# Lane rates, load distances, weight sums and a norm's factor moved in a Hymba encoder layer on one Trainium2 core

## The chip, the cores and the metric

The kernel runs on one core of one Trainium2 chip. The metric is the device time of one execution in microseconds (us), as the median of several runs; less is better. PE is the matmul engine (PEld its weight loads), DVE the vector engine, ACT the scalar engine, POOL the GpSimd engine, and SP the engine whose queue issues most DMA transfers.

## The reference

One layer of a bidirectional encoder for 1024 sample tokens and 256 prompt tokens of width 2048. The two requests share the weights.

```python
hn = rms_norm(x, norm_g)
proj = hn @ w_in                      # 2048 -> 4896 columns
xbc, z_ssd, dt_raw, q, k, v, z_att, mq, z_mem = split_cols(proj, IN_SIZES)
xbc = silu(centred_dwconv(xbc, conv_w, conv_b))          # 5 taps
y = ssd_scan(forward) + ssd_scan(backward) + d_skip * xs  # chunks of 128, 16 heads of 64
yg = (y * silu(z_ssd)).reshape(b, T, 2, 512)
o_ssd = rms_norm(yg, ssd_norm_g)                          # 1024 columns
o_att = window_attention(q, k, v, sink) * silu(z_att)     # 8 heads of 64, 2 kv heads, |t-s| <= 128
mk, mv = split_cols(rms_norm(mem) @ w_mem_kv)
o_mem = softmax(mq @ mk.T) @ mv * silu(z_mem)             # 4 heads of 128, 256 memory rows
return x + concatenate([o_ssd, o_att, o_mem]) @ w_out
```

## The kernel before

**Products.** A product in fp32 is made as three matmuls on operands split into a high and a low part (`wh`, `wl` of the weights, `xH`, `xL` of the activations). A weight tile comes by DMA into `wraw`; `wsplit` makes `wh` on ACT (L206) and `wl` on DVE (L207). The ten token tiles of 128 rows (eight of the sample, two of the prompt) form two groups of five.

**Main blocks.** `block_tok` (matmuls at L258 to L260, 512 columns wide) has the tokens on the partitions and five accumulators `acc`; `block_feat` (L293 to L295, 320 wide) has the features there. `block_pair` (L1236 to L1238) makes a pair of products as seven instead of eight, with sums of weight tiles that `weight_sums` forms on POOL (L1208) from tiles loaded at L1201. In order of time stand: the memory's keys and values; the q block of group 0; the pairs with the input weights; the k, v, dt block and the z and x blocks; the same kind of blocks for group 1; the "o" blocks with the output weights; and the last pairs. A block yields once for each of its 16 steps in depth.

**Lanes.** Beside the main blocks two lanes of generators hold the small work. Lane 0 holds key preparation, window attention (`attn`) and memory attention (`mem_attn`) by tile; lane 1 the row statistics, `dt_prep`, and the scan's two passes (`ssd_up`, `ssd_down`). After each block step `pump` adds the block's two rates from `RATES` (lane 0, lane 1) to what is owed, and takes that many steps of each lane. A `yield` in a lane's generator is the end of such a step. So a number in `RATES` and the number of `yield`s between two operations together say how many block steps, and matmuls, lie between these operations in the program.

**From program to order.** The program order is not the order of the engines: a list scheduler places each instruction by its dependences, the buffers' lives and priorities (`tc.high_priority`), and may bring a transfer forward; `tc.issue_after(marks)` ties some instructions to the last weight split.

**Names used below.** In `attn`: `q` (loaded at L599, squared into `sq` at L602), `qh` (its halves), `pq` (turned in PSUM at L623), `qT` (copied by ACT at L625), `psc` (scores, L641 and L642), `nm` (minus maximum, from DVE at L643), `lg` and `pT` (probabilities, and turned ones, L664). In `mem_attn`: `mq`, `pmq` (turned at L717), `sq` (L722), `mqh` and `mql` (high and low part, L730 on ACT and L732 on DVE), `pms` (scores, L745 to L747), `mpr` (probabilities, L754 and L759), `pmt` (turned, L767). In the scan: `pst` (a chunk's state, L868 to L870), `bh`, `fh`, `fl`, `bth`, `btl` (high and low parts for it, `fh` and `bh` by ACT at L882 among others), `rf` and `rb` (decays, L925 and L931), `py` (a chunk's product, L942), `pyb` (the backward part, L1063), `yd` (the sum), `yss` and `yrs` (sum of squares, and the norm's factor for two groups of 512 columns), `so` (the turned result, L1012).

**The norm of the scan's output.** `ssd_down` squares half of y (`scale=0.5`), takes the root's inverse by `rsqrt` on POOL, multiplies it by 0.5 on POOL (L1081), and leaves the tile in `last_y`. `norm_ssd`, called in the next tile's generator, multiplies the two halves of y by it on DVE (L1001), and `turn_ssd` turns and stores them.

**Refills of the activations' operand.** `run` drives a block. It also takes pieces from `pend`: a piece is loaded by DMA (L188) into one of four buffers `ch`, and some steps later split into `xH` (L197 or L200 on ACT) and `xL` (L198 or L201 on DVE). In each step the oldest loaded piece is split if `lag` of them are in hand, and then one more is loaded. The pieces of the output operand come from `oT` this way: two quads during the second zm block, two during the first "o" block.

Of the kernel before, what the change touches and what calls it, by code (L numbers as in the profile page):

```python
# [16 lines left out]
ALU = mybir.AluOpType  # L17
# [12 lines left out]
RBB = 4  # L30

RATES = ({'kv': (4.0, 1.0), 'z1': (2.2, 1.7)},
         {'kv': (1.5, 1.5), 'x': (2.1, 2.15), 'q': (2.25, 2.5), 'za': (2.15, 2.5), 'z0': (2.1, 2.5),
          'z1': (2.1, 2.55), 'mq': (2.0, 2.7), 'zm': (1.75, 2.75), 'o': (2.15, 2.4)})
FAR = 1e30

UNITS = (0, 8, 1, 9, 2, 10, 3, 11, 4, 12, 5, 13, 6, 7)
# [7 lines left out]
def hymba_encoder_kernel(  # L45
# [7 lines left out]
    V, A, G, T, S = nc.vector, nc.scalar, nc.gpsimd, nc.tensor, nc.sync  # L53
# [361 lines left out]
    def w2(name):  # L415
        return mp.tile([P, 512], F32, tag="wa", name=name, bufs=WA)
# [172 lines left out]
    def attn(t):  # L589
# [8 lines left out]
        q = w2("q")  # L598
        S.dma_start(q, q_d[t])  # L599
        yield  # L600
        sq = w2("sq")
        A.activation(sq, q, AF.Square)  # L602
        ss = sm.tile([P, 8], F32, tag="s8", name="qss", bufs=4)
# [99 lines left out]
    def mem_attn(t):  # L703
# [4 lines left out]
        if grp == 0:  # L708
            S.dma_start(hv(q, 4), mT_d[:, :, tc_])
        else:  # L710
            S.dma_start(q, mq_d[t])
        yield

        def turned():
# [281 lines left out]
    def norm_ssd():  # L996

        if "y" in last_y:
            t, ys, rs = last_y.pop("y")
            for g in range(2):  # L1000
                V.tensor_scalar(out=ys[g], in0=ys[g], scalar1=rs[:, g:g + 1], scalar2=None, op0=ALU.mult)  # L1001
                last_y[g] = t, ys[g]

    def turn_ssd(g):
# [10 lines left out]
    def ssd_down(t):  # L1015
        first = t in (0, NS)
        last = t in (NS - 1, NT - 1)
        tok = slice(t * P, (t + 1) * P)
        ss = sm.tile([P, 2], F32, tag="s2", name="yss", bufs=4)
        if not last:  # L1020
            cc = mp.tile([P, 2, P], F32, tag="btok", name="cc", bufs=1)
            S.dma_start(cc, xbc_d[10:12, :, tok].rearrange("f p c -> p f c"))
        ld = []
        for g in range(2):
            c = slice(g * 512, (g + 1) * 512)

            y = mp.tile([P, 512], F32, tag="ya" if t % 2 else "rf", name="yd", bufs=2)
            S.dma_start(y, yp_d[t][:, c])
            if g == 0 and t < 5:
                z = mp.tile([P, 512], F32R, tag="xs", name="zd", bufs=2)  # L1030
                S.dma_start(hv(z.bitcast(F32), 4), yT_d[:, :, tok])
            else:
                z = mp.tile([P, 512], F32, tag="xs", name="zd", bufs=2)
                S.dma_start(z, z_d[g][t])
            st = None
            if not first:
                st = state[:, c] if last else wb("st2")
                S.dma_start(st, sb_d[t][:, c])
            d = mp.tile([P, 4, P], F32R, tag="rb", name="ydT", bufs=RBB)
            S.dma_start(d.bitcast(F32), yd_d[t][:, 4 * g:4 * g + 4, :])  # L1040
            ld.append((y, z, st, d))

        def diag_in(g):
            ps = psum("pd")
            for j in range(4):
                T.transpose(ps[:, j * P:(j + 1) * P].bitcast(F32R), ld[g][3][:, j, :], identr)
            V.tensor_add(ld[g][0], ld[g][0], ps)

        for _ in range(9 if last else 4):
            yield  # L1050
        norm_ssd()
        diag_in(0)
        yield
        for g in range(2):
            c = slice(g * 512, (g + 1) * 512)
            y, z, st, _ = ld[g]
            if g == 0 and t < 5:
                zr, z = z, psum("pz")
                for j in range(4):
                    T.transpose(z[:, j * P:(j + 1) * P].bitcast(F32R), zr[:, j * P:(j + 1) * P], identr)  # L1060
            if not last:
                pf = psum("pyb")
                T.matmul(pf, cc[:, g, :], state[:, c], start=True, stop=True)  # L1063
                y2 = wb("y3")
                V.tensor_mul(hv(y2), hv(pf), hb(eacs_all[:, t, 16 + 8 * g:24 + 8 * g], 8, 64))
                V.tensor_add(y, y, y2)
            V.tensor_mul(y, y, z)
            if g == 0 and t < 5:
                z = wb("zq")
            A.activation(z, y, AF.Square, scale=0.5, accum_out=ss[:, g:g + 1])  # L1070
            if not first and not last:
                V.tensor_mul(hv(state[:, c]), hv(state[:, c]), hb(cd_all[:, t, 16 + 8 * g:24 + 8 * g], 8, 64))
                V.tensor_add(state[:, c], state[:, c], st)
            yield
            turn_ssd(g)
            if g == 0:
                diag_in(1)
                yield
        rs = sm.tile([P, 2], F32, tag="s2", name="yrs", bufs=4)
        rsqrt(rs, ss, 1.0 / 512, 2)  # L1080
        G.tensor_scalar(out=rs, in0=rs, scalar1=0.5, scalar2=None, op0=ALU.mult)  # L1081
        last_y["y"] = t, [x[0] for x in ld], rs
        yield
        if first:
            for _ in range(3):
                yield
            norm_ssd()
            yield
            yield
            for g in range(2):  # L1090
                turn_ssd(g)
                yield
# [204 lines left out]
    def p_step(j):  # L1297
        if j == 9:
            need(x_rows, [0])
        with ExitStack() as st:  # L1300
            for ins in marks:
                st.enter_context(tc.issue_after(ins))
            if j in (25, 27):
                weight_sums(w_in_pairs, (j - 25) // 2)
            for f, k in sorted(p_plan.get(j, ()), key=lambda x: ((p_split, p_sums, p_fill, p_load).index(x[0]), x[1])):
                f(k)

# [92 lines left out]
    def run(gen, rates, after=None, hold=0, lag=2, extra=None):  # L1400

        for k in gen:
            if after is not None:
                pend.extend(after(k))
            if hold:
                for _ in range(2 if k < KT - 4 else 0):
                    if pend:
                        u = pend.popleft()()
                        next(u)
                        next(u)  # L1410
            else:

                if loaded and (len(loaded) == lag or not pend or k >= KT - 4):
                    next(loaded.popleft())
                if pend and k < KT - 4:
                    loaded.append(pend.popleft()())
                    next(loaded[-1])

            if k >= hold:
                pump(rates)  # L1420
            if extra is not None:
                extra(k)
# [99 lines left out]
    run(block_tok(w_mem_rows(1), 4, ev_mv, places=TURNED), MR[1], extra=p_step)  # L1522

    def tok(name, w, evac, after=None, grp=0):
        run(block_tok(w, 5, evac), RATES[grp][name], after)

    def feat(name, b, evac, grp, after=None, extra=None):
        run(block_feat(f"{name}{b}", evac), [r / 2 for r in RATES[grp][name]], after, lag=3, extra=extra)

    run(block_tok(w_in_rows("q"), 5, ev_raw(q_d, 0), feats=PAIRED, places=PAIRED), (0, 0),  # L1530
        extra=lambda k: p_step(16 + k))
# [197 lines left out]
```

## The time and the profile before

| | |
|---|---|
| median of 3 runs | 1786.98 us (1786.98 to 1789.12) |
| profiled execution | 1787.15 us, span 1785.4 us |
| granted clock of PE | 1.00 in every stretch |
| DMA moved | 301.12 MB, 169 GB/s on the mean |
| HBM | 236.36 MB read, 62.69 MB written |

The span runs from the first to the last instruction that the profiler recorded; 1.75 us of the execution's time lie around it. Lines of the profile are read so. In the list of waits, "PE psc L641 <- ACT qT L625: 0.5, 1, 0.5" says that the matmuls of line 641 that write psc waited for ACT's instruction of line 625 that writes qT: 0.5 us in all, once, 0.5 us at the longest. In the timeline, a row has the start, the duration, the engine, the line, the operation, out<-in by the program's names, the shapes and a count, and in brackets the idle time of the engine before it and what ended that. In a list by tile, the three figures are the least, the median and the greatest duration in ns, and then the first and the last start. Matmuls are pipelined: the distance between two starts says more than a matmul's own duration.

### The profile page before, as it was taken

The numbers are of one execution on the slowest core, as the hardware profiler recorded it, in microseconds if no ns is written. First come the engines' busy times: TensorE is split into PE (matmuls) and PEld (weight loads), VectorE is DVE, ScalarE is ACT, GpSimd is POOL, SyncE is SP. The second block draws the span as 40 slices with busy tenths as digits, with TensorE's granted clock in tenths as the row PEclk, the third lists the DMA queues.
The fourth block names the chain that finished last, engine by engine and source line by source line (L and its number), as shares of the span: only waits on it lengthen the run. The fifth ranks groups of instructions, "written<-read, shape, count | busy, mean of one in ns | idle before, by whom it ended". The sixth has DMA issues, their size and how long they took to land.

```text
span 1785.4 us, 31407 instructions
## 1 busy us (share of the span) xinstructions
PE 1774.2 (99%) x10838; PEld 1605.7 (90%) x10838; DVE 1245.6 (70%) x2358; ACT 921.0 (52%) x2049; POOL 542.2 (30%) x900
## 2 busy tenths in 40 slices
PE   9999999999999999999999999999999999999999
PEld 8888999999998999999889977877988888899999
DVE  5595788888868887778665665556777644766665
ACT  5554455554435766656464565544447533533333
POOL 0105789989710101001001000000100000058775
PEclk9999999999999999999999999999999999999999
DMA  8554454445446644453645645547777764744442
GB/s 305 188 180 124 136 153 148 141 144 162 124 145 211 196 136 138 130 162 112 192 115 172 193 148 165 168 157 250 227 227 239 241 194 140 224 143 148 148 141 78
DMA packets 208208, 301.12 MB, mean 169 GB/s; under 512 B 19569, under 2 KB 86193, under 8 KB 208049
## 3 DMA queue, kind: packets, MB, share of 16 engines
q1 hardware_dynamic: 207904, 299.06, 54.4%
q8 instruction: 85, 1.39, 0.3%
q14 instruction: 75, 0.61, 0.1%
q10 hardware_dynamic: 144, 0.06, 0.0%
HBM read 236.36 MB, written 62.69 MB: 167 GB/s over the span
## 4 chain that ended last, share of the span: by engine, by line
PE 88%; issue 6%; DVE 2%; DMA 2%; ACT 1%; POOL 1%; SPq 0%; ACTq 0%; POOLq 0%; DVEq 0%
PE acc L258 10%; PE acc L259 10%; PE acc L260 10%; PE acc L1238 7%; PE acc L1236 7%; PE acc L1237 7%; PE acc L293 5%; PE acc L295 5%; PE acc L294 5%; PE accm L1237 3%; PE accm L1236 3%; PE accm L1238 3%; PE po L673 1%; PE ppt L663 1%; PE py L942 1%
## 5 line engine op out<-in xcount | busy, mean ns | idle before, releaser
L207 DVE TENSOR_TENSOR wl<-wraw,wh 128x512 fp32r<-128x512 f32 (+1 forms) x480 | 345.4, 721 | 241.0 <-ACT wh L206 234.2
L206 ACT ACTIVATE wh<-wraw 128x512 fp32r<-128x512 f32 (+1 forms) x480 | 292.1, 613 | 307.0 <-PE acc L260 150.4
L258 PE MATMUL acc<-wh,xH 128*128 128x512 f32 (+1 forms) x1088 | 418.7, 385 | 0.2 <-DVE v_all L337 0.2
L259 PE MATMUL acc<-wl,xH 128*128 128x512 f32 (+1 forms) x1088 | 409.7, 377 | 1.1 <-DVE wl L207 1.1
L260 PE MATMUL acc<-wh,xL 128*128 128x512 f32 (+1 forms) x1088 | 410.1, 377 | 0.0
L259 PEld LDWEIGHTS acc<-wl,xH 128*128 128x128 f32 x1088 | 204.6, 188 | 37.7 <-DVE wl L207 2.2
L258 PEld LDWEIGHTS acc<-wh,xH 128*128 128x128 f32 x1088 | 204.5, 188 | 37.7 <-issue 3.3
L260 PEld LDWEIGHTS acc<-wh,xL 128*128 128x128 f32 x1088 | 204.2, 188 | 36.7 <-issue 0.2
L293 PE MATMUL acc<-xH,wh 128*128 128x320 f32 x640 | 202.7, 317 | 0.0
L206 ACT ACTIVATE sh<-ws 128x384 fp32r<-128x384 f32 x176 | 91.4, 523 | 209.0 <-POOL ws L1208 117.1
L294 PE MATMUL acc<-xL,wh 128*128 128x320 f32 x640 | 198.9, 311 | 0.0
L295 PE MATMUL acc<-xH,wl 128*128 128x320 f32 x640 | 198.0, 309 | 0.0
L207 DVE TENSOR_TENSOR sl<-ws,sh 128x384 fp32r<-128x384 f32 x176 | 124.7, 712 | 98.0 <-ACT sh L206 97.7
L1208 POOL TENSOR_TENSOR ws<-wraw 128x128 f32<-128x128 f32 x176 | 110.7, 629 | 212.5 <-DMA wraw<-in_w_in_pairs_dram 92.7
L635 POOL COPY lg<-nsink 128x2 f32<-128x2 f32 x40 | 13.7, 341 | 377.1 <-PE ppt L663 243.6
L293 PEld LDWEIGHTS acc<-xH,wh 128*128 128x128 f32 x640 | 120.2, 188 | 2.6 <-issue 2.2
L294 PEld LDWEIGHTS acc<-xL,wh 128*128 128x128 f32 x640 | 120.3, 188 | 1.7 <-issue 1.4
L295 PEld LDWEIGHTS acc<-xH,wl 128*128 128x128 f32 x640 | 120.2, 188 | 0.6 <-issue 0.5
L1208 POOL TENSOR_TENSOR ws<-wraw,ws 128x128 f32<-128x128 f32 x176 | 116.3, 661 | 13.8
L1208 POOL TENSOR_TENSOR wraw<-wraw 128x128 f32<-128x128 f32 x176 | 110.9, 630 | 13.7
L1208 POOL TENSOR_TENSOR ws<-ws,wraw 128x128 f32<-128x128 f32 x176 | 115.0, 654 | 0.0
L362 DVE SCALAR_TENSOR_TENSOR c<-u,vec,c 128x638 f32<-128x638 f32 (+1 forms) x96 | 90.1, 939 | 9.0 <-ACT c L357 8.6
(437 smaller groups left out, 3942.9 us busy)
## 6 DMA issues: line engine op xcount, KB each, us to landing
wraw<-in_w_in_laid_dram SPq DMA_DIRECT2D x176, 256.0 KB, 2.9
wraw<-in_w_in_pairs_dram SPq DMA_DIRECT2D x112, 256.0 KB, 2.7
wraw<-in_w_out_laid_dram SPq DMA_DIRECT2D x64, 256.0 KB, 3.6
wraw<-in_w_out_pairs_dram SPq DMA_DIRECT2D x64, 256.0 KB, 2.8
rf<-ac SPq DMA_DIRECT2D x40, 256.0 KB, 4.1
rb<-ac SPq DMA_DIRECT2D x40, 256.0 KB, 5.0
wraw<-in_w_mem_laid_dram SPq DMA_DIRECT2D x32, 256.0 KB, 4.2
xst<-in_x_sample_dram SPq DMA_DIRECT2D x20, 256.0 KB, 5.3
```

The source lines that it names most:

```text
L206: a = A.activation(h, raw, AF.Copy)
L207: b = V.tensor_sub(l, raw, h.bitcast(F32))
L258: T.matmul(ps[t][:, :n], sh, h[:, :n], start=(k_ == 0), stop=False)
L259: T.matmul(ps[t][:, :n], sh, l[:, :n], start=False, stop=False)
L260: T.matmul(ps[t][:, :n], sl, h[:, :n], start=False, stop=(k_ == KT - 1))
L293: T.matmul(o, sh, cur["H", q][:, m, c], start=(k == 0), stop=False)
L294: T.matmul(o, sh, cur["L", q][:, m, c], start=False, stop=False)
L295: T.matmul(o, sl, cur["H", q][:, m, c], start=False, stop=(k == KT - 1))
L1208: G.tensor_tensor(out=o, in0=x, in1=y, op=op)
L1236: T.matmul(ps[p], h, xh, start=(k_ == 0), stop=False)
L1237: T.matmul(ps[p], h, xl, start=False, stop=False)
L1238: T.matmul(ps[p], l, xh, start=False, stop=(k_ == 7))
```

## The change

Five edits. The rates of lane 0 in the blocks of `RATES[1]` rise by 2 to 9%; those of lane 1 stay. `attn` and `mem_attn` get one more `yield` between the load of q or mq and its first use. The factor 0.5 of the scan's norm goes from its own POOL instruction into a second scalar of DVE's product. The first two calls of `weight_sums` with the input pairs stand at steps 21 and 23 of the pair plan in place of 25 and 27. The lag of refills is 3 in place of 2 in `block_tok` blocks, and 4 in place of 3 in `block_feat` blocks.

```diff
 RATES = ({'kv': (4.0, 1.0), 'z1': (2.2, 1.7)},
-         {'kv': (1.5, 1.5), 'x': (2.1, 2.15), 'q': (2.25, 2.5), 'za': (2.15, 2.5), 'z0': (2.1, 2.5),
-          'z1': (2.1, 2.55), 'mq': (2.0, 2.7), 'zm': (1.75, 2.75), 'o': (2.15, 2.4)})
+         {'kv': (1.6, 1.5), 'x': (2.2, 2.15), 'q': (2.3, 2.5), 'za': (2.25, 2.5), 'z0': (2.2, 2.5),
+          'z1': (2.2, 2.55), 'mq': (2.1, 2.7), 'zm': (1.9, 2.75), 'o': (2.25, 2.4)})
...
         S.dma_start(q, q_d[t])
         yield
+        yield
         sq = w2("sq")
...
             S.dma_start(q, mq_d[t])
+        yield
         yield
...
-                V.tensor_scalar(out=ys[g], in0=ys[g], scalar1=rs[:, g:g + 1], scalar2=None, op0=ALU.mult)
+                V.tensor_scalar(out=ys[g], in0=ys[g], scalar1=rs[:, g:g + 1], scalar2=0.5, op0=ALU.mult, op1=ALU.mult)
...
         rsqrt(rs, ss, 1.0 / 512, 2)
-        G.tensor_scalar(out=rs, in0=rs, scalar1=0.5, scalar2=None, op0=ALU.mult)
         last_y["y"] = t, [x[0] for x in ld], rs
...
-            if j in (25, 27):
-                weight_sums(w_in_pairs, (j - 25) // 2)
+            if j in (21, 23):
+                weight_sums(w_in_pairs, (j - 21) // 2)
...
-        run(block_tok(w, 5, evac), RATES[grp][name], after)
+        run(block_tok(w, 5, evac), RATES[grp][name], after, lag=3)
...
-        run(block_feat(f"{name}{b}", evac), [r / 2 for r in RATES[grp][name]], after, lag=3, extra=extra)
+        run(block_feat(f"{name}{b}", evac), [r / 2 for r in RATES[grp][name]], after, lag=4, extra=extra)
```

At the weights, the rows of the engines' orders are the same: SP's queue has the first transfer of L1201 (L1202 in the changed kernel) at the same place. On PE, lane groups move by about one block step from the x blocks on. The first place to see is memory tile 7 on PE, where L717 turns its query (pmq) and L745 onward makes its scores (pms); before, the scores come some thirty block matmuls later than the turn:

```order
L258 MATMUL acc<-wh,xH_16293 128x512
L259 MATMUL acc<-wl,xH_16293 128x512
L260 MATMUL acc<-wh,xL_16294 128x512
L745 MATMUL pms<-mkH,mqh 128x256
L746 MATMUL pms<-mkL,mqh 128x256
```

Now, where lines of this function are two further down, the scores come four matmuls behind the turn:

```order
L719 MATMUL pmq<-identr,mq 128x128 x4
L258 MATMUL acc<-wh,xH_15669 128x512
L259 MATMUL acc<-wl,xH_15669 128x512
L260 MATMUL acc<-wh,xL_15670 128x512
L258 MATMUL acc<-wh,xH_15669 128x512
L747 MATMUL pms<-mkH,mqh 128x256
```

So the scores have moved some 28 matmuls nearer to the turn. The second place is attention tile 5 on PE, where L623 turns half a query (pq) and L641 and L642 make the scores (psc); before, fifteen block matmuls stand between, and these are the last:

```order
L258 MATMUL acc<-wh,xH_6938 128x512
L259 MATMUL acc<-wl,xH_6938 128x512
L260 MATMUL acc<-wh,xL_6939 128x512
L641 MATMUL psc<-kT,qT 128x384
L642 MATMUL psc<-kL,qT 128x384
L641 MATMUL psc<-kT,qT 128x384
```

Now three matmuls of the scan (pst) stand between:

```order
L260 MATMUL acc<-wh,xL_6939 128x512
L624 MATMUL pq<-identr,qh 128x128 x4
L870 MATMUL pst<-bh,bth 128x512
L871 MATMUL pst<-bl,bth 128x512
L872 MATMUL pst<-bh,btl 128x512
L642 MATMUL psc<-kT,qT 128x384
```

So the second turn of that query has moved behind the block matmuls, next to the scores.

The third place is ACT's queue where it makes fh, the high part of a scan operand (L882), beside the splits of the operand's pieces (L200), the memory probabilities (L754), a weight split (L206) and the decays (L925); before:

```order
L754 ACTIVATE mpr,mden<-pms,mm,mr 128x256 x2
L831 ACTIVATE cb<-pcb 128x256
L754 ACTIVATE mpr,mden<-pms,mm,mr 128x256 x2
L200 ACTIVATE xH_16109<-chd,vec 128x640 x2
L206 ACTIVATE wh<-wraw 128x512
L200 ACTIVATE xH_16109<-chd,vec 128x640 x2
L925 ACTIVATE rf<-rf,wj_all 128x128 x4
L882 ACTIVATE fh<-xf 128x512
```

Now:

```order
L206 ACTIVATE wh<-wraw 128x512
L200 ACTIVATE xH_16140<-chd,vec 128x640
L833 ACTIVATE cb<-pcb 128x256
L756 ACTIVATE mpr,mden<-pms,mm,mr 128x256 x2
L200 ACTIVATE xH_16140<-chd,vec 128x640
L206 ACTIVATE wh<-wraw 128x512
L884 ACTIVATE fh<-xf 128x512
L200 ACTIVATE xH_16140<-chd,vec 128x640
L927 ACTIVATE rf<-rf,wj_all 128x128 x4
```

So the decays and a split have moved from ahead of fh to behind it.

## The prediction, before the result was known

> **What bounds the kernel now.** I read the page's head first, then the busy time in stretches, then the waits of the matmul engine, and last the timeline at each of them. The head gives the span, and each engine's busy time with its share and its number of instructions:
>
> ```profile
> span 1785.4 us, 31407 instructions
> PE 1774.2 (99%) x10838; PEld 1605.7 (90%) x10838; DVE 1245.6 (70%) x2358; ACT 921.0 (52%) x2049; POOL 542.2 (30%) x900
> ```
>
> PE is busy for 99% of the span. The order of PE's instructions holds the same matmuls in both kernels; the first one that stands elsewhere in the changed kernel is executed at 607 us now, and behind about 1500 us nothing moves any more. So the stretches are cut there, and two narrower ones are added for later use:
>
> ```profile
> core 0: us, PE busy (x) PEld busy (x) DVE busy (x) ACT busy (x) POOL busy (x), PEclk, DMA share, GB/s
> 0.00:607.00 607.00, 604.34 (x3666) 567.10 (x3667) 463.10 (x767) 314.07 (x637) 320.25 (x515) 1.00 0.55 168
> 607.00:1500.00 893.00, 888.03 (x5455) 771.83 (x5454) 596.13 (x1294) 492.64 (x1212) 71.62 (x129) 1.00 0.57 175
> 1500.00:1785.40 285.40, 281.83 (x1721) 266.78 (x1719) 186.38 (x299) 114.25 (x200) 150.32 (x256) 1.00 0.48 149
> 1180.00:1320.00 140.00, 138.62 (x844) 116.61 (x841) 100.39 (x211) 63.87 (x155) 16.26 (x37) 1.00 0.68 212
> ```
>
> In the 893 us that can move at all, PE is idle for 893.00 − 888.03 = 4.97 us, at a granted clock of 1.00. The change takes no matmul away, so what it can win is among these waits, and what it can lose is a new wait of the same kind. In the list of PE's waits (total us, times, longest) these lead in that stretch:
>
> ```profile
> PE pmt L767 <- DVE mpr L759: 1.3, 2, 1.2
> PE pyb L1063 <- ACT so L1012: 0.9, 1, 0.9
> PE pst L868 <- ACT fh L882: 0.8, 1, 0.8
> PE pms L747 <- DVE mql L732: 0.6, 1, 0.6
> PE psc L641 <- ACT qT L625: 0.5, 1, 0.5
> PE pd L1046 <- DVE nm L643: 0.5, 1, 0.5
> ```
>
> They are few and single. A wait also costs somewhat more than its row says, because a busy PE is not PE at its peak:
>
> ```profile
> 726.85 0.40 PE L870 MATMUL pst<-fh,btl 128*128 128x512 f32 x1
> 727.09 0.34 PE L641 MATMUL psc<-kT,qT 128*128 128x384 f32 x1
> 727.26 0.34 PE L642 MATMUL psc<-kL,qT 128*128 128x384 f32 x1
> 728.11 0.45 PE L641 MATMUL psc<-kT,qT 128*128 128x384 f32 x1 [0.51 <-ACT qT L625]
> ```
>
> Two such matmuls start 727.26 − 727.09 = 0.17 us apart when nothing is in the way, and here 728.11 − 727.26 = 0.85 us, so 0.68 us is lost where the row says 0.51, a third more. All PE idle time between 607 and 1500 us is then worth 4.97 to about 6.6 us.
>
> **The change part by part.** *Paired weights fetched sooner.* The transfer is L1201, called from two steps of the pair plan that lie four steps earlier now.
>
> ```profile
> 56.99 0.43 SPq L1201 DMA_DIRECT2D wraw<-in_w_in_pairs_dram  x1
> ```
>
> It goes out at 56.99 us, far ahead of the q block in which the code stands, because the scheduler had already brought it forward. In the new order it stands at the same row of SP's queue, and POOL's sums at the same rows too. Cost and gain: 0. The same holds for all else before 607 us.
>
> *One more lane step between load and use.* The transfers concerned are q and mq, with ACT as the engine that waits:
>
> ```profile
> ACT sq L602 <- DMA q<-q: 5.5, 3, 2.5
> ACT sq L722 <- DMA mq<-mq: 4.0, 2, 2.9
> ```
>
> In SP's new order the ten q loads stand within three rows of their old places, and their first use on ACT moves by 0 to 13 rows, by none or by fewer than five in eight of the ten; the mq loads and uses move as little. The raised rates take back what the extra step gives. ACT has idle time (492.64 of 893 us busy), so its 9.5 us of waits cost PE nothing except where a PE row names ACT, and the one that follows from such a load (pyb behind so, the second row of the list above) keeps its neighbours on ACT, SP and PE. I leave it at 0.
>
> *Pieces of the output operand.* With a longer lag the piece isn't loaded sooner: one is loaded in each step, and filled when three (or four) are in hand rather than two (or three). The splits on ACT and DVE come a step later, with four buffers in the ring as before. Bounds: from −0.8 us to +0.8 us, the size of the one PE wait that the splits take part in:
>
> ```profile
> 1341.91 0.83 ACT L200 ACTIVATE xH<-chd,vec 128x640 fp32r<-128x640 f32 x1 [0.64 <-DMA chd<-oT]
> 1342.64 0.61 ACT L206 ACTIVATE wh<-wraw 128x512 fp32r<-128x512 f32 x1
> 1343.16 1.54 ACT L200 ACTIVATE xH<-chd,vec 128x640 fp32r<-128x640 f32 x2
> 1344.61 1.27 ACT L925 ACTIVATE rf<-rf,wj_all 128x128 f32<-128x128 f32 x4
> 1345.77 0.62 ACT L882 ACTIVATE fh<-xf 128x512 fp32r<-128x512 f32 x1
> 1346.44 0.50 PE L868 MATMUL pst<-fh,bth 128*128 128x512 f32 x1 [0.76 <-ACT fh L882]
> ```
>
> PE waits 0.76 us for fh (the upper half of a state operand), which stands behind splits and four decay products on ACT. In ACT's new order (shown with the change) the decay products and one of the splits stand behind fh, so I take this wait as gone: −0.8 us.
>
> *The norm's half.* The POOL product is removed in all ten tiles; its factor goes into a second scalar of the DVE product L1001.
>
> ```profile
> DVE yd L1001 <- POOL yrs L1081: 18.2, 10, 3.5
> 1190.65 0.70 POOL L124 TENSOR_TENSOR yrs<-yrs,mhalf 128x2 f32<-128x2 f32 x1
> 1191.44 0.23 POOL L1081 TENSOR_SCALAR yrs<-yrs 128x2 f32<-128x2 f32 x1
> 1191.70 0.49 DVE L1001 TENSOR_SCALAR yd<-yd,yrs 128x512 f32<-128x512 f32 x1 [3.46 <-POOL yrs L1081]
> L1001 DVE TENSOR_SCALAR yd<-yd,yrs x20: 470/484/522, 1191.7 to 1500.8; 128x512 f32<-128x512 f32 x20
> L759 DVE TENSOR_SCALAR mpr<-mpr,mden x40: 333/348/356, 826.7 to 1464.9; 128x256 f32<-128x256 f32 x40
> ```
>
> DVE starts 0.26 us behind the POOL product's start; without it, about 0.3 us sooner, 3 us of DVE waiting over ten tiles. The form with two scalars exists already (L759): 348 ns for 256 columns, against 484 ns for 512 in the old form. Two of the former for one of the latter would be 0.21 us more, 4 us of DVE over the 20 products; with one instruction's fixed part in place of two it is near nothing, which I take. What DVE wins reaches PE only where PE waits for DVE: PE is idle for 1.38 us in all of 1180 to 1320 us. Between +1.4 and −1.4 us; I take −0.4, since DVE wins a little and no leading wait names this chain. The Trainium skill's page "Perfetto Trace Analysis", section "Identifying the Most-Contended Engine", speaks against a large gain here: the engine with the highest occupancy is to be improved first, and POOL and DVE are not that. The same section calls the busy time of matmuls a bad measure and takes that of the weight loads instead, which is 771.83 of 893 us here, so that up to 121 us would be open for a better order; the trace speaks against this, since 512-wide matmuls that wait for nothing start 0.24 us apart (726.85 to 727.09) and their loads can't fill that.
>
> *Higher rates.* Groups of lane matmuls are moved by a block step or so, about 3.5 us of PE time. Some of PE's old waits stand where this happens:
>
> ```profile
> 853.14 0.52 PE L767 MATMUL pmt<-identr,mpr 128*128 128x128 f32 x3 [1.16 <-DVE mpr L759]
> 1242.40 0.70 PE L1063 MATMUL pyb<-state,cc 128*128 128x512 f32 x1 [0.90 <-ACT so L1012]
> 1365.08 0.39 PE L747 MATMUL pms<-mkH,mql 128*128 128x256 f32 x1 [0.62 <-DVE mql L732]
> 1401.88 0.41 PE L767 MATMUL pmt<-identr,mpr 128*128 128x128 f32 x2 [0.16 <-DVE mpr L759]
> ```
>
> The two longest (1.16 us at 853, 0.90 at 1242) keep their neighbours on PE and on the engines that they wait for, and stay. At 1365 us one transfer less stands ahead on SP; half goes, −0.3. The pair at 1401 us moves apart, −0.2. Against that stand new short distances. In attention tile 5 the scores (psc) stood 15 block matmuls behind the turned queries that they read (pq), and now three matmuls are left between, as the rows with the change show. This happens in tiles 4 to 7, while tiles 8 and 9 lose such a place. What it costs in the places that have it:
>
> ```profile
> PEld psc L641 <- ACT qT L625: 1.9, 5, 0.8
> ```
>
> A mean of 1.9 / 5 = 0.38 us, from near 0 to 0.8. Four new less two old: +0.8 at the mean; I take +0.4, because the three matmuls cover part. In the same way, in memory tiles 7 and 8 the scores (pms) come four block matmuls behind the turned queries (pmq), where it was some thirty in tile 7. Four block matmuls at 0.24 us give 1.0 us, in which ACT's mqh must land (an estimate of 0.6 us, the 0.62 of fh's split of the same shape). If ACT and DVE are free, nothing is lost; with a queue ahead, up to about 0.9 us each (0.62 by the row at 1365 us, and a third more). I take 0.25 each, +0.5. Last, the memory scores stand nearer to their turns (pmt) in five or so tiles (by the two orders, with PE's times from the trace, some 4 to 6 us where it was 5 to 9); bounds 0 and 1.16 us each by the row at 853 us. The bulk is still wide enough: +0.5.
>
> The sum: −0.8 − 0.4 − 0.3 − 0.2 + 0.4 + 0.5 + 0.5 = −0.3 us. The profiled execution took 1787.15 us (span 1785.4 and 1.75 around it), 0.17 above the median of 1786.98 us. So 1786.9 us against 1787.15, or 1786.7 against the median; I give 1786.9.
>
> **The rivals.** *The waits go (faster).* If the moves take away not three but nearly all of the stretch's PE waits, 4.97 to 6.6 us are won: 1782.2 to 1780.5 us. For it: the waits are single events, each at a place where a queue happened to be long, and 178 pieces on PE have moved. Against: the two longest (853 and 1242 us) keep their order. Chance 0.29.
>
> *The queues of ACT and DVE come due too soon (slower).* A higher rate puts the consumer nearer to the producer on PE, while ACT and DVE serve the same producer behind weight splits. If every shortened place stalls in full: four scores by 0.8, two memory scores by 0.9, five turns by 1.16, together 10.8 us, less the 1.7 won: 1796 us; with half of them 1791.7 us. It decides from the point where over half of the new short places wait for more than 0.8 us. For it: DVE's 596 of 893 us, and the wait of 1.16 us behind mpr that exists at the old rates. Against: five short score places cost 0.38 us on the mean. Chance 0.26.
>
> *It does not do what it says.* The loads and their first uses hold their places, the weights' fetch too, and only single waits differ. That is what I forecast: 1786.9 us, chance 0.45.
>
> **How the numbers follow.** About 0.2%, 3.6 us, is what a measurement of this kernel can tell from no change. Faster by more needs 72% of all PE idle time from 607 to 1500 us (3.57 of 4.97) to go, or new room that I don't see: 0.29. Slower by more needs some five stalls of 0.8 us: 0.26. The rest is 0.45. The range reaches from 1780.0, all idle time gone at the dearer price, to 1794.0, about three quarters of the stalls.
>
> **What would show it.** Right: PE's waits between 607 and 1500 us sum to 4 to 6 us, no row for pst behind fh at 1346 us, the 853 us wait still 1.2 us, L1201 still at 57 us, DVE's row for L1001 now behind L124 and 3 us smaller. Wrong: rows of PE waiting for qT, mqh, mql or mpr that sum to over 4 us (slower), or PE busy for all but 2 us of the stretch (faster); and any change before 607 us, or behind 1500 us, would break the reading that the order there decides.

## The result: slower by 0.44%

The changed kernel takes 1795.49 us (median of 6 runs, 1793.36 to 1798.86), and the kernel before 1787.26 us (6 runs). The ratio is 1.0044, interval [1.0034, 1.0054]: about 8 us slower, and 1.5 us above the upper end of the range. The profiled execution took 1795.68 us, 0.19 above the median. The head of its page and the busy time in three stretches:

```profile
span 1794.0 us, 31400 instructions
PE 1777.7 (99%) x10838; PEld 1606.4 (90%) x10838; DVE 1246.7 (69%) x2358; ACT 921.7 (51%) x2049; POOL 539.1 (30%) x890
...
0.00:607.00 607.00, 602.91 (x3649) 565.13 (x3650) 459.97 (x763) 313.71 (x636) 320.66 (x515) 1.00 0.54 168
607.00:1180.00 573.00, 569.54 (x3644) 505.35 (x3642) 392.43 (x874) 337.28 (x841) 43.90 (x74) 1.00 0.50 155
1180.00:1510.00 330.00, 324.87 (x1835) 270.27 (x1835) 209.56 (x427) 156.06 (x375) 24.24 (x45) 1.00 0.66 206
```

The last two stretches of the kernel before:

```profile
607.00:1180.00 573.00, 570.96 (x3656) 506.84 (x3656) 390.64 (x880) 338.90 (x847) 46.64 (x75) 1.00 0.51 155
1180.00:1510.00 330.00, 327.08 (x1851) 273.30 (x1848) 208.37 (x420) 156.33 (x371) 24.98 (x54) 1.00 0.67 209
```

PE is idle for 3.46 + 5.13 = 8.59 us from 607 to 1510 us, where it was 2.04 + 2.92 = 4.96 us. The matmuls of the main blocks come in one and the same order in both kernels, so the start of the n-th of these 8880 can be compared:

| n-th block matmul | before, us | after, us | late by |
|---|---|---|---|
| 3600 | 610.9 | 613.4 | 2.6 |
| 5000 | 913.7 | 915.7 | 2.0 |
| 5800 | 1114.9 | 1119.4 | 4.5 |
| 6400 | 1281.5 | 1286.3 | 4.8 |
| 6600 | 1328.8 | 1335.3 | 6.4 |
| 7200 | 1507.6 | 1516.2 | 8.6 |
| last | 1781.5 | 1790.1 | 8.5 |

Six of the 8.5 us (8.6 − 2.6) are lost between 607 and 1508 us: half a microsecond is won up to 914 us, then two and a half are lost up to 1115 us and nearly four from 1281 us on. That is more than the 3.6 us that idle rows gained. By the one wait that the prediction measured, a wait costs a third more than its row says, which would make 4.8 us of them; what the rest is, is not known. The 2.6 us ahead of 607 us lie where the two programs hold the same instructions in the same order; they belong to this execution and not to the change (the last section). The waits of PE from 607 to 1510 us are now (total us, times, longest):

```profile
PE pmt L769 <- DVE mpr L761: 2.0, 3, 1.0
PE pd L1048 <- DMA ydT<-yd: 1.7, 1, 1.7
PE pmo L784 <- ACT mpT L773: 1.2, 1, 1.2
PE pxs L863 <- ACT cb L833: 1.1, 1, 1.1
PE pyb L1065 <- ACT so L1014: 0.7, 1, 0.7
PE psc L642 <- ACT qT L626: 0.5, 1, 0.5
```

The wait for fh is gone, and so is that at 1365 us. In their place stand a load (ydT, an operand of the scan's second pass), mpT (the turned memory probabilities) and cb. None of the three is a distance that the prediction had counted as shortened. All three can be followed back. First cb, ACT and PE at 1348 us, in the timeline:

```profile
1341.56 0.63 ACT L206 ACTIVATE wh<-wraw 128x512 fp32r<-128x512 f32 x1 [2.59 <-issue]
1347.29 0.83 ACT L200 ACTIVATE xH<-chd,vec 128x640 fp32r<-128x640 f32 x1 [5.10 <-DMA chd<-oT]
1348.02 0.36 ACT L833 ACTIVATE cb<-pcb 128x256 f32<-128x256 f32 x1
1348.44 0.54 PE L863 MATMUL pxs<-identr,xc 128*128 128x128 f32 x4 [1.09 <-ACT cb L833]
```

ACT waits 5.10 us for the first piece of a quad of the output operand, and cb stands behind this piece. In the kernel before, cb stood ahead of the same piece, and the wait for it was 0.31 us (the 0.64 us in the prediction is the second piece's):

```profile
1338.64 0.38 ACT L831 ACTIVATE cb<-pcb 128x256 f32<-128x256 f32 x1
...
1340.43 0.83 ACT L200 ACTIVATE xH<-chd,vec 128x640 fp32r<-128x640 f32 x1 [0.31 <-DMA chd<-oT]
```

The wait for chd<-oT is one round trip: the store of so, issued at 1338.02 us, takes 5.30 us, and the load behind it 3.94 us. Before, the two took 4.30 and 4.53 us, nearly as long together, so the round trip is not what grew: ACT now comes to the piece with cb and the memory probabilities still to do. Then ydT, on SP and PE:

```profile
1292.47 0.53 SPq L1015 DMA_DIRECT2D oT<-so  x1
1293.05 0.62 SPq L1042 DMA_DIRECT2D ydT<-yd  x1
1298.52 0.51 PE L1048 MATMUL pd<-identr,ydT 128*128 128x128 f32 x4 [1.72 <-DMA ydT<-yd]
```

The load is issued behind a second store of so, for which SP's queue waited 0.9 us, and takes 5.3 us. In the kernel before this load was issued ahead of that store, 5.9 us ahead of its use; it took 4.5 us, and PE did not wait for it:

```profile
1286.26 0.44 SPq L1040 DMA_DIRECT2D ydT<-yd  x1
1286.92 0.52 SPq L1013 DMA_DIRECT2D oT<-so  x1
```

Last mpT, on PE and ACT:

```profile
940.90 1.03 PE L769 MATMUL pmt<-identr,mpr 128*128 128x128 f32 x8
...
942.70 0.64 ACT L773 ACTIVATE mpT<-pmt 128x512 f32<-128x512 f32 x1
...
943.39 0.82 PE L784 MATMUL pmo<-mpT,mv 128*128 128x128 f32 x5 [1.16 <-ACT mpT L773]
```

No load is waited for here. ACT works without a break from 937.58 us on, and mpT stands behind four probabilities, four copies of a block's result, a decay product and a weight split. It starts 1.80 us behind the turn; before, it was 0.74 us, with the same two block matmuls between turn and use on PE.

### The profile page after: what moved, and what is told of

Same layout as the page of the kernel before. It is cut to its first block, busy times and chain, and to the rows that moved or that the text cites. A ratio compares the mean times of both kernels' runs of the same rounds, so it can differ in the third digit from the quotient of the medians.

```text
span 1794.0 us, 31400 instructions
## 1 busy us (share of the span) xinstructions
PE 1777.7 (99%) x10838; PEld 1606.4 (90%) x10838; DVE 1246.7 (69%) x2358; ACT 921.7 (51%) x2049; POOL 539.1 (30%) x890
## 3 DMA queue, kind: packets, MB, share of 16 engines
q8 instruction: 85, 1.39, 0.3%
## 4 chain that ended last, share of the span: by engine, by line
PE 81%; POOL 5%; issue 5%; DVE 4%; DMA 3%; ACT 1%; SPq 0%; POOLq 0%; DVEq 0%; ACTq 0%
PE acc L258 10%; PE acc L260 10%; PE acc L259 10%; PE acc L1239 6%; PE acc L1237 6%; PE acc L1238 6%; PE acc L293 5%; PE acc L295 5%; PE acc L294 5%; POOL ws L1209 3%; PE accm L1238 2%; PE accm L1237 2%; PE accm L1239 2%; PE po L674 1%; PE ppt L664 1%
## 5 line engine op out<-in xcount | busy, mean ns | idle before, releaser
L206 ACT ACTIVATE wh<-wraw 128x512 fp32r<-128x512 f32 (+1 forms) x480 | 292.4, 613 | 316.6 <-PE acc L260 154.0
L206 ACT ACTIVATE sh<-ws 128x384 fp32r<-128x384 f32 x176 | 91.3, 523 | 212.2 <-POOL ws L1209 111.5
```

Of the source, the lines that this page charges most:

```text
L206: a = A.activation(h, raw, AF.Copy)
```

## The experiments

The first four runs do one edit each. Ratios are to the kernel before, measured on the same chip.

**The lag alone.**

```diff
-        run(block_tok(w, 5, evac), RATES[grp][name], after)
+        run(block_tok(w, 5, evac), RATES[grp][name], after, lag=3)
...
-..., after, lag=3, extra=extra)
+..., after, lag=4, extra=extra)
```

> Of the five edits only the longer lag of the refills (3 and 4 in place of 2 and 3). Theory A (the changed kernel's named waits): the longer lag is what puts a split that waits for its piece (ACT waits 5.1 us for chd<-oT at 1342 us in the changed kernel, 0.64 before) ahead of cb and the memory probabilities on ACT, so this alone costs +2 to +3 us and shows PE waiting for cb or mpr near 1350 us. Theory B (scatter of the order): PE's order holds two rows out of place here, so within 1 us of before. Theory C (rates too high): within 1 us too, as no rate changes.

Ratio 0.9995 [0.9987, 1.0004]. The lag by itself costs nothing. Theory A's reading that the lag put the piece ahead of cb is wrong: with the lag alone, cb runs at 1340.61 us, ahead of the piece at 1342.79 us.

**The norm alone.**

```diff
-...scalar1=rs[:, g:g + 1], scalar2=None, op0=ALU.mult)
+...scalar1=rs[:, g:g + 1], scalar2=0.5, op0=ALU.mult, op1=ALU.mult)
...
-        G.tensor_scalar(out=rs, in0=rs, scalar1=0.5, scalar2=None, op0=ALU.mult)
```

> Only the norm's factor moved into the DVE product. No matmul stands elsewhere. All theories: within 1 us of before, -0.4 by the prediction; DVE waits for yrs fall by about 3 us.

Ratio 0.9994 [0.9985, 1.0002]. DVE's waits for yrs and the products' durations, in a list of waits and a list by tile of this run:

```profile
DVE yd L1001 <- POOL yrs L124: 14.5, 9, 3.2
...
L1001 DVE TENSOR_SCALAR yd<-yd,yrs x20: 479/482/490, 1191.3 to 1498.6; 128x512 f32<-128x512 f32 x20
```

The waits fall from 18.2 to 14.5 us, and the product with two scalars takes 482 ns against 484 ns: the second scalar is free.

**The rates alone.** The two lines of `RATES` from the change.

> Only the raised rates of lane 0. Theory A: the late ydT load (1.7 us of PE at 1298 us), pmo behind mpT (1.2 us at 943) and the psc place at 681 come from the rates: +4 to +6 us. Theory B: 1931 rows of PE stand elsewhere than before, against 639 in the full change, so it costs as much as the full change or more, +6 to +12 us, at other places than the full change. Theory C: the shortening of every distance is the cost and the extra lane step gives part back, so +8 to +12 us.

Ratio 1.0027 [1.0017, 1.0037], about 5 us. The waits for ydT (1.4 us) and for an mpT (0.6 us, at 926 us and not at 943) are there, none for cb, and a longer one that the full change doesn't have:

```profile
1367.72 0.58 PE L745 MATMUL pms<-mkH,mqh 128*128 128x256 f32 x1 [3.53 <-ACT mqh L730]
```

The size fits theory A; B and C both asked for more.

**The extra lane steps alone.**

```diff
         S.dma_start(q, q_d[t])
         yield
+        yield
...
             S.dma_start(q, mq_d[t])
+        yield
         yield
```

> Only the extra lane step behind the loads of q and mq. Theory A: the waits named come from rates and lag, so within 2 us of before. Theory B: 1556 rows of PE stand elsewhere, so +4 to +10 us although every first use has more room. Theory C: more room from load to use, so -1 to -3 us.

Ratio 1.0008 [1.0000, 1.0017]: at most a little slower, though 1556 rows of PE stand elsewhere. B's "every shift is dear" is too strong, and C's gain doesn't come. The four edits alone add to 0.27 + 0.08 − 0.05 − 0.06 = 0.24%, where the full change costs 0.44%; with intervals of about 0.09% to each side of five numbers this gap is at the edge of chance. PE changes between block and lane matmuls 424 times from the 3600th to the 7200th block matmul here (408 before, 426 in the full change), in the same 896.7 us as before, so more changes by themselves are not the cost.

One of the full change's places is made here: the piece already stands ahead of cb on ACT. ACT waits 0.99 us for it, and PE 1.01 us behind cb, at 1336 us.

The next four take a part out, or turn it round.

**Without the rates.** The full change with before's `RATES`.

> The full change with before's rates. The rates alone cost 5.2 us, the extra lane steps 1.5, the lag 0 and the norm -1. If the edits add up (theory A): 1787.5 to 1788.5 us, about before, and no PE wait for ydT near 1298 us. If the cost is any shift of the lane groups (theory B, 1559 rows of PE out of place): +3 us or more.

Ratio 1.0009 [1.0000, 1.0019]. The raised rates are the cause of some 6 of the 8 us. The extra steps, the lag, the norm and the weights together are worth what the extra steps are worth alone.

**Without the lag.** The full change with before's two lags.

> The full change with before's lag. The lag alone costs nothing, but in the full change the split on ACT waits 5.1 us for its piece at 1342 us and holds up cb and the memory probabilities (PE: 1.1 and 1.0 us). If lag and rates are dear only together (theory A): 2 to 3 us faster than the full change. If the lag is free there too (theory B): within 1 us of the full change.

Ratio 1.0037 [1.0025, 1.0050], not to be told from the full change. ACT waits 4.68 us for its piece in this kernel too, so the lag does not set that place. Nor do the rates by themselves: with the rates alone, cb runs at 1342.09 us, ahead of the piece at 1343.95 us. The extra lane steps turn the two round (the piece is ahead, at a wait of 0.99 us, with them alone, and at 1.33 us without the rates), and with the raised rates on top the wait becomes 4 us or more.

**The rates lowered.**

```diff
-         {'kv': (1.5, 1.5), 'x': (2.1, 2.15), 'q': (2.25, 2.5), 'za': (2.15, 2.5), 'z0': (2.1, 2.5),
-          'z1': (2.1, 2.55), 'mq': (2.0, 2.7), 'zm': (1.75, 2.75), 'o': (2.15, 2.4)})
+         {'kv': (1.4, 1.5), 'x': (2.0, 2.15), 'q': (2.2, 2.5), 'za': (2.05, 2.5), 'z0': (2.0, 2.5),
+          'z1': (2.0, 2.55), 'mq': (1.9, 2.7), 'zm': (1.6, 2.75), 'o': (2.05, 2.4)})
```

> Before with the lane 0 rates of the second group lowered by about as much as the change raises them, nothing else. Theory B (the order of before is a chosen one, and any shift of lane groups against the blocks costs): +3 to +8 us, as much as raising. Theory C (a higher rate shortens distances and is dear for that): within 1 us of before, or faster by up to 2 us.

Ratio 1.0012 [1.0004, 1.0021]. Lower is dearer as well, by 2 us against 5 for higher. Neither B (+3 to +8) nor C (no loss) holds in full.

**The late rates taken back.**

```diff
-          'z1': (2.2, 2.55), 'mq': (2.1, 2.7), 'zm': (1.9, 2.75), 'o': (2.25, 2.4)})
+          'z1': (2.2, 2.55), 'mq': (2.0, 2.7), 'zm': (1.75, 2.75), 'o': (2.15, 2.4)})
```

> The full change with before's rates in the blocks mq, zm and o only. In the full change 3.9 us are lost between 1300 and 1500 us and about 2 between 930 and 1180. Theory A: the part from 1180 us on comes from the rates there, so some 3 to 4 us faster than the full change, 1791 to 1792 us. Theory B: lane groups stay shifted by what the earlier blocks took up, so the late waits come in other places and at about the same sum: within 2 us of the full change.

Ratio 1.0019 [1.0010, 1.0028]: over half of the loss goes, as theory A had it. The ydT wait is not in this run's list; those for mpT (1.2 us) and cb (1.0 us) are, so these two do not come from the late rates.

The next two runs try to take the named waits away in the full change. PE's order stays as it is, but for two rows in the second run.

**The load of ydT sooner.**

```diff
-            S.dma_start(d.bitcast(F32), yd_d[t][:, 4 * g:4 * g + 4, :])
+            with tc.high_priority(offset=60):
+                S.dma_start(d.bitcast(F32), yd_d[t][:, 4 * g:4 * g + 4, :])
```

> The full change, with a higher priority for the load of ydT: on SP it now stands ahead of the store of so and of the tile's other loads; no instruction of PE, DVE, ACT or POOL stands elsewhere. Theory A (named waits): PE's wait of 1.7 us for ydT at 1298 us goes, so 2 us faster than the full change, 1793.5 us. Rival: another load or store that was pushed back by it ends the same place, and the time stays at 1795.5 us.

Ratio 1.0042 [1.0029, 1.0054]: nothing is won. The ydT wait is gone, and the longest waits of PE in the run are others:

```profile
PE pyb L1066 <- ACT so L1014: 2.4, 1, 2.4
...
PE pxs L863 <- ACT cb L833: 1.8, 1, 1.8
```

The first, in the timeline of ACT and PE:

```profile
1248.13 0.63 ACT L603 ACTIVATE sq<-q 128x512 f32<-128x512 f32 x1 [4.01 <-DMA q<-q]
1248.66 0.58 ACT L1014 ACTIVATE so<-pr 128x512 f32<-128x512 f32 x1
1249.29 1.12 PE L1066 MATMUL pyb<-state,cc 128*128 128x512 f32 x2 [2.40 <-ACT so L1014]
```

The same place in the full change, where sq and so stand in the same order:

```profile
1246.01 0.63 ACT L603 ACTIVATE sq<-q 128x512 f32<-128x512 f32 x1 [2.33 <-DMA q<-q]
1246.55 0.58 ACT L1014 ACTIVATE so<-pr 128x512 f32<-128x512 f32 x1
1247.18 0.70 PE L1065 MATMUL pyb<-state,cc 128*128 128x512 f32 x1 [0.72 <-ACT so L1014]
```

ACT waits for q, the load to which the change meant to give time, and so stands behind it, for which PE waits. Sooner ydT loads are not needed for the longer wait: in the run with o alone back, whose engines hold the full change's order up to 1356 us, ACT waits 3.60 us for this q.

**Three places at once.** The same for ydT, and higher priority (60) for the copies cb and mpT on ACT.

```diff
-        A.activation(cb, hv(ps[:, :256], 2), AF.Copy)
+        with tc.high_priority(offset=60):
+            A.activation(cb, hv(ps[:, :256], 2), AF.Copy)
...
-            A.activation(pT, pt, AF.Copy)
+            with tc.high_priority(offset=60):
+                A.activation(pT, pt, AF.Copy)
```

> The full change, with a higher priority for three instructions: the load of ydT, the copy cb on ACT, and the copy mpT on ACT. Two rows of PE stand elsewhere. Theory A: the waits for ydT (1.7 us at 1298), cb (1.1 at 1348) and mpT (1.2 at 943) go, each worth a third more than its row: 4 to 5 us faster than the full change, 1790.5 to 1791.5 us. Theory B (any loss comes back at the next place): within 2 us of the full change.

Ratio 1.0045 [1.0033, 1.0057]. The wait for ydT fell to 0.4 us, that for mpT stayed at 1.2 us, and pmt behind mpr (2.5 us) and pyb behind so (2.1 us) lead the list. The higher priority did not do its work on ACT: cb still stands behind the piece (1348.69 behind 1347.95 us), and mpT behind the same copies and weight split. The wait for cb went only because the piece cost ACT 4.01 us in this execution. So of theory A, that the loss is these three waits and goes with them, only the part on ydT was put to the test, here and in the run before, and there the time did not follow.

**The same three in the kernel before.** The same lines, in the kernel before.

> The kernel before with the same three priorities, as the control. It has none of the three waits, so by theory A within 1 us of before. If the three priorities win 3 us or more here too, they say nothing of the change.

Ratio 1.0008 [1.0000, 1.0017]: they win nothing there either.

**The two free edits.** The norm and the lag together.

> Before with the two edits that cost nothing by themselves, the norm's factor and the longer lag: 0 to -2 us against before (alone they gave -1.1 and -0.9 us, both within their intervals).

Ratio 0.9999 [0.9991, 1.0008]. No version here beats the kernel before.

**The stores off SP's queue.**

```diff
-            S.dma_start(oT_d[2 + g][t // 5][:, :, t % 5 * P:(t % 5 + 1) * P], hv(o, 4))
+            G.dma_start(oT_d[2 + g][t // 5][:, :, t % 5 * P:(t % 5 + 1) * P], hv(o, 4))
```

> The full change, with the 20 stores of so issued from POOL's queue instead of SP's; no matmul stands elsewhere. Theory D (loads that PE waits for stand behind these stores in SP's in-order queue, as ydT did at 1298 us): the ydT wait goes and, as nothing is pushed back on SP, 2 to 4 us are won, 1791.5 to 1793.5 us. Theory E (the distances on PE between a lane's producer and consumer are the cost, whatever the queue): within 1 us of the full change, 1795.5.

Ratio 1.0089 [1.0076, 1.0102]. The control:

> The kernel before with the same stores on POOL's queue, as the control. Both theories: within 1.5 us of before, since no PE wait there ends on a load behind such a store.

Ratio 1.0056 [1.0044, 1.0068], so the pair doesn't tell D from E: the cure is dear by itself, and the forecast for the control, within 1.5 us, missed by 8 us. Its waits, from 1180 to 1510 us in the control, show why:

```profile
POOL oT L1013 <- ACT so L1012: 69.3, 10, 12.5
...
DVE yd L1001 <- POOL yrs L1081: 28.1, 10, 5.7
```

POOL now stands waiting for so, with the norm's factor queued behind; DVE's waits for it rise from 18.2 to 28.1 us. PE has a new wait of 1.5 us behind such a yd. It is the same fault on another queue: an instruction that waits holds up one that PE needs.

The last four ask which late rate is dear.

**zm alone back.** In the full change, `'zm': (1.75, 2.75)` for `(1.9, 2.75)`.

> The full change with the rate of the zm blocks alone at 1.75 instead of 1.9 (the largest raise, 8.6%); 56 rows of PE move. Rates of mq, zm and o together were worth 4.4 us of the full change. If the size of the raise decides: -3 us or more. If each shift costs about alike: -1 to -2 us.

Ratio 1.0047 [1.0035, 1.0059]. The largest raise costs nothing that can be measured, and neither forecast held.

**The late rates alone.** In the kernel before, mq 2.1, zm 1.9 and o 2.25.

> Before with only the rates of mq, zm and o raised (PE unchanged up to row 7025, about 1250 us). If the late rates cost by themselves: +4 us, as they did within the full change. If they cost only on top of what the earlier rates and the extra lane steps have shifted: within 1.5 us of before.

Ratio 1.0027 [1.0016, 1.0037], from 1787.36 to 1795.39 us over nine runs: they cost by themselves, and as much as all the raised rates alone (1.0027).

**o alone back.** In the full change, `'o': (2.15, 2.4)` for `(2.25, 2.4)`.

> The full change with only the rate of the o blocks taken back (2.15); PE moves from about 1345 us on (156 rows), and the waits at 943 and 1298 us stay. Taking back mq, zm and o together won 4.4 us, zm alone nothing. If o is the dear one: 3 to 4 us faster than the full change. If single parts can't be told apart (each shift only deals the waits anew): within 1.5 us.

Ratio 1.0035 [1.0022, 1.0047], between the two. Up to 1356 us its order on PE is that of the full change, and yet its profile shows pyb waiting 1.98 us behind so (0.72 there), and pd 2.5 us (1.72 there), behind a DVE product in the list, while the load of ydT takes 6.1 us and lands at the same time. The order sets where a wait can come; the landing of the loads sets how long it is.

**mq alone back.** In the full change, `'mq': (2.0, 2.7)` for `(2.1, 2.7)`.

> The full change with only the rate of the mq block taken back (2.0); PE moves from about 1250 us on (164 rows). If mq is the dear one: the ydT wait of 1.7 us at 1298 us goes and 3 to 4 us are won. If single parts can't be told apart: within 1.5 us of the full change.

Ratio 1.0024 [1.0014, 1.0035]: by the medians nearly half of the loss is this one rate, 5%, in one block; by the two intervals it is anything from an eighth to three quarters. Its stretch:

```profile
1180.00:1510.00 330.00, 327.09 (x1848) 272.54 (x1848) 209.76 (x428) 156.26 (x374) 24.93 (x45) 1.00 0.66 208
```

PE is idle for 2.91 us of it, as in the kernel before (2.92), where the full change has 5.13. PE's order differs from the full change's from 1185 to 1315 us (not from 1250 us on, as was expected). In this run's list of waits none for ydT, pyb or cb is left, and on ACT sq, at 1251 us now, no longer waits for its load. So with mq back PE no longer waits at ydT and pyb. The other engines' orders at ydT and cb did not change back, though: ydT still goes out behind a store of so (1290.90 behind 1290.33 us), and the piece still stands ahead of cb, at a wait of ACT of 4.07 us, which is just short enough for PE (the table in the next section). The mpT wait at 943 us (0.9 us here) lies ahead of that block and stays.

## Why the prediction was wrong

**What held.** Six of the 8.5 us lie between 607 and 1508 us, where the prediction looked for them. The weights' transfer is issued where it was (56.37 us after, 56.99 before) and nothing can come of it by the order (this edit wasn't run alone, since it leaves every engine's order as it was). The norm's fold saves 3.5 us of DVE's waits and its second scalar is free; in time it is about −1 us, within its interval (−2.7 to +0.4 us). The lag is worth nothing that can be measured. The named terms came out near their sizes: fh's wait went, the 853 us wait stayed (0.81 us), behind qT there is one wait of 0.49 us, at 681 us in an earlier tile than the four counted, and behind mql at 1442 us, by the distance of the starts, one of some 0.2. Its range for PE's waits, 4 to 6 us, was passed: they sum to 8.6 us.

**What failed.** The step that failed is the sentence on ACT's waits for its loads: that they "cost PE nothing except where a PE row names ACT", with pyb left at 0 because its neighbours stand still. The sum priced new waits only where a distance on PE had shrunk; a producer that is late because of what stands ahead of it in its own engine's queue had no term. The profile has 1.72 us (ydT behind a store on SP), 1.09 us (cb behind a piece on ACT) and 1.16 us (mpT behind ACT's own work, with no load) instead, about 4 us of PE rows against a forecast sum of −0.3 us. I looked at the rows between fh and its piece, saw the decays move behind fh, and booked a gain of 0.8 us; in the same rows the piece had moved ahead of cb and of the memory probabilities, and its wait went from 0.31 to 5.10 us.

How ACT's wait reaches PE can be read from the runs that hold these two places (waits in us):

| run | ACT for q, 1246 us | PE behind so | ACT for the piece, 1347 us | PE behind cb |
|---|---|---|---|---|
| the full change | 2.33 | 0.72 | 5.10 | 1.09 |
| without the lag | 2.64 | 1.02 | 4.68 | 0.69 |
| zm alone back | 2.82 | 1.21 | 5.41 | 1.42 |
| o alone back | 3.60 | 1.98 | 5.58 | 1.58 |
| ydT sooner | 4.01 | 2.40 | 5.78 | 1.79 |
| three places | 3.71 | 2.10 | 4.01 | none |
| stores off SP | 3.78 | 2.16 | 7.24 | 3.25 |

In every row PE waits 1.6 us less than ACT at the first place and 4.0 us less at the second. So in these runs each place has a fixed slack, up to which ACT's wait costs PE nothing, and beyond it PE pays in full. The kernel before has the first place too (2.51 and 0.90 us, again 1.6 apart). The prediction saw this link and left it at 0 because the neighbours stand still; the same neighbours give 0.72 to 2.40 us here, as the load lands.

The waits of ACT for DMA from 1180 to 1510 us, before:

```profile
ACT xH L197 <- DMA chd<-oT: 4.1, 1, 4.1
ACT sq L722 <- DMA mq<-mq: 4.0, 2, 2.9
ACT sq L602 <- DMA q<-q: 2.5, 1, 2.5
```

And after:

```profile
ACT sq L724 <- DMA mq<-mq: 9.7, 3, 4.8
ACT xH L200 <- DMA chd<-oT: 5.1, 1, 5.1
ACT xH L197 <- DMA chd<-oT: 4.0, 1, 4.0
...
ACT sq L603 <- DMA q<-q: 2.3, 1, 2.3
```

The waits for mq more than double, in a change that was to give these loads a step more; in this execution no PE row follows from them. The second omission is of the same kind, on SP: I counted the places of the q and mq loads there, and not those of the other loads that the shift moves, ydT's among them.

**The rivals.** The slower one had the sign, and its price with half of the places stalled or all (1796 us) encloses the result; for half, 10.8 / 2 − 1.7 gives 1790.9 us and not 1791.7, which halves the 1.7 us won as well. That the result falls between is luck as far as the listed places go: the short distances hardly stall, and the rows for qT, mqh, mql and mpr that were to sum to over 4 us sum to about 3. Its words "the queues of ACT and DVE come due" fit mpT at 943 us, where ACT is behind with its own work; at cb a queue holds a row that waits for DMA ahead of a row that PE needs. The range, with three quarters of the stalls as the upper end, was 1.5 us short.

**What stays open.** That the rates cause some 6 us, and that mq's is part of it, is shown by taking them back. That ACT's waits for loads are charged to PE at the places of pyb and cb is shown by the table. That the whole loss goes with the waits named is not shown: with ydT freed, other waits came up and the time stayed, and no run of the full change put cb or mpT sooner on ACT. The runs fit an order in which many places have little slack left; beyond the two places measured this is argued. Why the early rates and the extra steps cost more together than apart, if they do, is answered in part: the wait for mpT at 943 us is in no run that has only one of the two, and the wait of 4 us or more ahead of cb came only with both.

## What to carry to other kernels

When a change shifts work between in-order queues, list for each row that waits for a DMA what stands directly behind it and who waits for that, before and after; the distance between a producer and its consumer on the bound engine says little without what stands ahead of the producer in its own queue. Where a wait of one engine shows in the other's row, their difference is the slack of that place, and it says what a longer wait will cost. Rates that interleave side work with a saturated engine can have a narrow best place: here 5% on one block cost, by the medians, nearly half a loss of 0.44%, and 2 to 9% lower was slower too, while nearly 9% on the zm blocks cost nothing that could be measured. A transfer that the code issues earlier is sooner only if the order of its queue says so.

## What was not expected of the hardware

PE's clock falls behind waits much shorter than I had thought worth a term. At 141 us the full change's PE waited 1.39 and 0.56 us for a weight split, in a stretch where PE's order equals that of the kernel before; there, the waits were 0.54 and 0.57 us, and with zm alone back, where it is the same too, 0.39 and 0.57 us. What followed, in the timeline and in the stretches of 5 us (the third number from the end is the granted clock):

```profile
143.03 0.50 PE L259 MATMUL acc<-wl,xH 128*128 128x512 f32 x1 [1.39 <-DVE wl L207]
...
144.56 0.80 PE L259 MATMUL acc<-wl,xH 128*128 128x512 f32 x1 [0.56 <-DVE wl L207]
145.15 0.63 PE L260 MATMUL acc<-wh,xL 128*128 128x512 f32 x1
145.58 0.63 PE L258 MATMUL acc<-wh,xH 128*128 128x512 f32 x1
...
140.00:145.00 5.00, 3.05 (x12) 1.95 (x11) 4.67 (x8) 1.90 (x4) 1.87 (x4) 0.94 0.18 49
145.00:150.00 5.00, 5.00 (x17) 3.98 (x17) 0.11 (x1) 2.22 (x5) 3.54 (x8) 0.72 0.58 186
```

Matmuls that started 0.23 us apart now start 0.43 us apart, for about 3.4 us (what is missing from the two clocks, 0.06 and 0.28 of 5 us, is 1.7 us, at half the rate). In all, some 2.2 us are lost here, and these are most of the 2.6 us that the table shows ahead of 607 us. The same drop came behind waits of 2.40 us (0.66 in the next 5 us, with ydT sooner) and 3.53 us (0.76 and 0.90, with the rates alone), and none behind one of 3.23 us at 1356 us (1.00, stores off SP, control), none behind the full change's own 1.72 us at 1298 us, and in no run any behind one of 1.3 us or less. The Trainium skill's page "TensorE: Matmul & The Clock Gate", section "What's actually happening", has the gate pass half of the clock's pulses after an idle window of about 3.4 us that runs freely; the halved rate and the chance in it agree with these rows, while a single gap of 1.39 us, with 0.56 us behind it, was enough here.

It also bears on the spread. With the rates of mq, zm and o alone, the two fastest of nine runs took 1787.36 and 1788.81 us at a mean clock of 1.000, and the slowest 1795.39 at 0.998, which is 0.002 × 1795 = 3.6 us of clock, an estimate, as these clocks are given in thousandths. A change that adds waits of 1.5 to 3 us so pays for some of them twice, in some of its executions. For the full change this part is small: the mean clock of its six runs is worth 1.2 us, against 0.3 us for the kernel before in the runs beside the experiments, so about 0.9 of the 8 us.
